# Max-pooling by 16 along rows: two load slots that swing over a 9.5 KB gap, in place of three fixed ones

## The chip, the cores and the metric

The kernel runs on one core of a Trainium2 chip, with nothing else on it. The metric is the device time of one execution in microseconds (us). All timed runs were at a granted clock of 1.0. Ratios are computed as the mean time of one kernel's runs over the mean of the other's in the same rounds, so they are not quite the ratio of the medians that the text quotes. "Same" means within 2%.

## The reference

```python
# x: (32, 256, 4096) float32, output_size = 256
for i in range(output_size):
    start = int(i * length / output_size)
    end = int((i + 1) * length / output_size)
    result[:, :, i] = np.max(x[:, :, start:end], axis=-1)
```

Every output is the maximum of 16 neighbouring numbers: 134.22 MB are read, 8.39 MB are written. Per SBUF partition there are 16,384 outputs. The text calls one output with its 16 inputs (64 bytes) a *column*.

## The kernel before

One SBUF area per partition holds three load slots at its low end and the results at its high end. Results grow downwards into the space of the slots, so the loads shrink: one of 128 columns, two of 1,024, then three each of 1,000, 940, 884, 832 and 784, and at the end 736 and 152.

```python
slot_sizes = [MOST]                     # MOST = 1024 columns, 64 KB
rounds = [[FIRST] + [MOST] * (SLOTS - 1)]     # FIRST = 128, SLOTS = 3
# ... each later round: three loads of what the free room allows ...
for i, size in enumerate(loads):
    # ...
    at = n_loads % SLOTS * slot_sizes[n_loads // SLOTS] * W
    slot = area[:, at : at + size * W]
    nc.sync.dma_start(out=slot, in_=xg[:, a * W : b * W])
    nc.vector.reduce_max(
        out=area[:, base + a : base + b],
        in_=slot.rearrange("p (n w) -> p n w", w=W),
        axis=mybir.AxisListType.X,
    )
# ... after all loads: three stores, all on SyncE
for dst, src in stores:
    nc.sync.dma_start(out=dst, in_=src)
```

A load waits until the reduction that last read its slot is finished. With three slots, a load that is issued then has one whole load queued ahead of it and the rest of another moving.

Of the kernel before, what the change touches and what calls it, by code (L numbers as in the profile page):

```python
# [1 line left out]

# [4 lines left out]


@with_exitstack
def kernel(  # L10
    ctx: ExitStack,
    tc: tile.TileContext,
    x: bass.AP,
    output_size: bass.AP,
    out: bass.AP,
):





    nc = tc.nc
    P = nc.NUM_PARTITIONS
    fp32 = mybir.dt.float32

    B, C, L = x.shape
    O = int(output_size)
    assert L % O == 0, (L, O)
    W = L // O
    total = B * C * O // P  # L30
    assert B * C * O % P == 0

    AREA = 53200
    SLOTS = 3
    MOST = 65536 // (4 * W)
    ALIGN = 4
    FIRST = 128
    ROUNDS_A = 3
    LAST = 4


    slot_sizes = [MOST]
    rounds = [[FIRST] + [MOST] * (SLOTS - 1)]
    left = total - sum(rounds[0])
    while left:
        room = AREA - (total - left)
        n = min(room // (SLOTS * W + SLOTS) // ALIGN * ALIGN, MOST)
        if left <= slot_sizes[-1]:
            n = left
        slot_sizes.append(n)  # L50
        rounds.append([])
        while left and len(rounds[-1]) < SLOTS:
            n = min(n, left)
            rounds[-1].append(n)
            left -= n
    sizes = [n for r in rounds for n in r]
    groups = [sizes[: ROUNDS_A * SLOTS], sizes[ROUNDS_A * SLOTS :]]

    pool = ctx.enter_context(tc.tile_pool(name="pool", bufs=1))
    area = pool.tile([P, AREA], fp32, tag="area", name="area")  # L60

    xw = x.flatten_outer_dims().rearrange("r (o w) -> (r o) w", w=W)
    ow = out.flatten_outer_dims().rearrange("r o -> (r o)")

    stores = []
    n_loads = 0
    first = 0
    low = AREA
    for g, loads in enumerate(groups):
        n = sum(loads)  # L70
        xg = xw[first : first + P * n].rearrange("(p n) w -> p (n w)", p=P)
        og = ow[first : first + P * n].rearrange("(p n) -> p n", p=P)
        first += P * n
        base = low - n
        b = n
        for i, size in enumerate(loads):
            a = b - size
            at = n_loads % SLOTS * slot_sizes[n_loads // SLOTS] * W
            slot = area[:, at : at + size * W]
            nc.sync.dma_start(out=slot, in_=xg[:, a * W : b * W])  # L80
            nc.vector.reduce_max(  # L81
                out=area[:, base + a : base + b],
                in_=slot.rearrange("p (n w) -> p n w", w=W),
                axis=mybir.AxisListType.X,
            )
            n_loads += 1
            b = a
        low = base
        if g < len(groups) - 1:
            stores.append((og, area[:, base : base + n]))  # L90
        else:
            end = sum(loads[len(loads) - LAST :])
            for a, b in ((end, n), (0, end)):
                stores.append((og[:, a:b], area[:, base + a : base + b]))

    for dst, src in stores:
        nc.sync.dma_start(out=dst, in_=src)


# [1 line left out]
_INS = ['x', 'output_size']  # L101
_OUTS = [((32, 256, 256), 'float32')]

_NUMBERS = {'output_size': 256}


# [26 lines left out]
```

## Time and profile before

| before | |
|---|---|
| time, median of the first 3 runs | 335.2 us (335.14 to 335.36) |
| span of the profiled run | 333.4 us |
| bytes moved | 142.61 MB, 428 GB/s over the span |
| DMA queue, share of 16 engines' span | 99.1% |
| VectorE busy | 276.0 us (83%), 20 reductions |

Lines of the page of before: busy times, the DMA queue table (packets, MB, share of 16 engines' span), bytes, and the chain that ended last (DVE is VectorE, POOL is GpSimd, DMA a wait for a transfer).

```profile
span 333.4 us, 112 instructions
DVE 276.0 (83%) x20; POOL 0.2 (0%) x4
...
q1 hardware_dynamic: 3312, 142.61, 99.1%
HBM read 134.22 MB, written 8.39 MB: 428 GB/s over the span
...
DMA 64%; DVE 31%; DVEq 1%; another core or an unknown queue 0%; SPq 0%; issue 0%
```

The DMA engines are occupied throughout. VectorE's 31% in the chain are releases of slots, which hide under loads that are already queued; they cost nothing as long as the queue is never empty. A sign that it never is: the timeline of before from 60 to 102 us (start, duration, engine, line, what, and in brackets the idle time before it and who ended it; SPq is SyncE's sequencer, which issues):

```profile
44.26 17.22 DVE L81 TENSOR_REDUCE area<-area 128x1024 f32<-128x16384 f32 x1 [2.33 <-DMA area<-in_x_dram]
61.51 37.81 SPq L80 DMA_DIRECT2D area<-in_x_dram  x3
63.17 16.82 DVE L81 TENSOR_REDUCE area<-area 128x1000 f32<-128x16000 f32 x1 [1.69 <-DMA area<-in_x_dram]
82.14 16.82 DVE L81 TENSOR_REDUCE area<-area 128x1000 f32<-128x16000 f32 x1 [2.15 <-DMA area<-in_x_dram]
100.96 16.82 DVE L81 TENSOR_REDUCE area<-area 128x1000 f32<-128x16000 f32 x1 [2.00 <-DMA area<-in_x_dram]
```

A reduction starts when its load has landed, so the starts show the pace of the loads: 8.192 MB (128 partitions x 16,000 x 4 bytes) every 18.8 to 19.0 us, about 433 GB/s. The load issued at 61.51 us is not needed before 82.14 us, when the load that is queued ahead of it has come in too: 20.6 us in advance.

### The profile page before, as it was taken

To read this page: it belongs to the slowest core of one execution; us is meant where nothing else is said; L and a number is where in the kernel's file an instruction comes from. 1 tells how busy PE (TensorE), PEld (TensorE's weight loads), DVE (VectorE), ACT (ScalarE), POOL (GpSimd) and SP (SyncE) were. 2 spreads that over 40 slices of the span, in tenths; PEclk is the share of its full clock that TensorE was granted. 3 is DMA by queue.
4 is the path that set the end of the run, shared out by engine and by line. 5 is a ranking of instruction groups with operands and counts; after the bars stand their busy time and mean duration, and the time that the engine had idled before them with its cause. 6 is when DMAs were issued, how large, how long until landed. Compare 5 with 4: busy or idle time off the path is not lost.

```text
span 333.4 us, 112 instructions
## 1 busy us (share of the span) xinstructions
DVE 276.0 (83%) x20; POOL 0.2 (0%) x4
## 2 busy tenths in 40 slices
DVE  2009979797988989797989797989898898989990
POOL 0000000000000000000000000000000000000000
DMA  9898989898999998999999999999999999989997
GB/s 377 377 503 377 503 369 491 369 491 369 491 397 433 462 462 375 433 462 441 434 434 434 434 434 415 409 441 473 415 409 470 397 470 397 470 380 452 414 431 310
DMA packets 3312, 142.61 MB, mean 428 GB/s; under 512 B 368, under 2 KB 368, under 8 KB 368
## 3 DMA queue, kind: packets, MB, share of 16 engines
q1 hardware_dynamic: 3312, 142.61, 99.1%
HBM read 134.22 MB, written 8.39 MB: 428 GB/s over the span
## 4 chain that ended last, share of the span: by engine, by line
DMA 64%; DVE 31%; DVEq 1%; another core or an unknown queue 0%; SPq 0%; issue 0%
DMA area<-in_x_dram 64%; DVE area L81 31%; DVEq L128 1%; SPq L80 0%; DVEq L81 0%
## 5 line engine op out<-in xcount | busy, mean ns | idle before, releaser
L81 DVE TENSOR_REDUCE area<-area 128x1000 f32<-128x16000 f32 (+8 forms) x20 | 276.0, 13806 | 49.1 <-DMA area<-in_x_dram 49.1
L114 POOL MEMSET const-bfloat16-1.0<- 128x1 bf16 x1 | 0.1, 102 | 0.0
L114 POOL MEMSET const-uint8-127<- 128x1 uint8 x1 | 0.1, 101 | 0.0
L114 POOL MEMSET const-float32-0.0<- 128x1 f32 x1 | 0.1, 99 | 0.2 <-issue 0.2
L114 POOL MEMSET const-float32-1.0<- 128x1 f32 x1 | 0.1, 98 | 0.0
## 6 DMA issues: line engine op xcount, KB each, us to landing
area<-in_x_dram SPq DMA_DIRECT2D x3, 8000.0 KB, 40.1
area<-in_x_dram SPq DMA_DIRECT2D x3, 7520.0 KB, 37.5
area<-in_x_dram SPq DMA_DIRECT2D x3, 7072.0 KB, 35.3
area<-in_x_dram SPq DMA_DIRECT2D x3, 6656.0 KB, 33.2
area<-in_x_dram SPq DMA_DIRECT2D x3, 6272.0 KB, 31.3
area<-in_x_dram SPq DMA_DIRECT2D x1, 5888.0 KB, 30.3
out_dram<-area SPq DMA_DIRECT2D x1, 3998.0 KB, 27.6
out_dram<-area SPq DMA_DIRECT2D x1, 2966.0 KB, 34.2
```

The costliest lines, as they stand in the source:

```text
L81: nc.vector.reduce_max(out=area[:, base + a : base + b], in_=slot.rearrange("p (n w) -> p n w", w=W), axis=mybir.AxisListType.X,)
L114: nc = _bacc.Bacc("TRN2", target_bir_lowering=False, num_devices=1)
L128: with _tile.TileContext(nc) as tc:
```

## The change

Its intent is fewer and equal loads (17 instead of 20) of the largest row, 64 KB per partition, in two slots instead of three. Beside two 64 KB slots and the results some 19 KB per partition are left. That room becomes a gap of 152 columns (9.5 KB) at each slot: successive loads of a slot lie alternately at its low and at its high end. Two of them overlap in 872 of 1,024 columns only. The reduction is cut in two: first the 872 columns that the next load will overwrite, then the other 152. So the next load may be issued while the second part is still being reduced. The short first load (132 columns) lies in the first slot's gap, and the last results in the last slot.

```diff
-    SLOTS = 3
-    MOST = 65536 // (4 * W)
-    FIRST = 128
+    CHUNK = 1024
+    GAP = 152
+    FIRST = 132
+    LOADS_A, LOADS_B = 9, 6
...
+                low = n_loads % 2 * (CHUNK + GAP)
+                moved = n_loads // 2 % 2
+                at = low + moved * GAP
+                nc.sync.dma_start(out=ring[:, at * W : (at + n) * W], in_=xn)
+                if n == CHUNK:
+                    cut = CHUNK - GAP if moved else GAP
+                    parts = [(0, cut), (cut, n)]
+                    for u, v in parts if moved else parts[::-1]:
+                        pooled(dst[:, u:v], at + u, v - u)
+                else:
+                    end = (at + CHUNK) * W
+                    last_kept = ring[:, end - n : end]
+                    pooled(last_kept, at, n)
...
+        stores.append((og[:, 0:full], kept[:, base : base + full]))
...
+    stores.append((og[:, full : full + last], last_kept))
     for dst, src in stores:
         nc.sync.dma_start(out=dst, in_=src)
```

`pooled` is the `reduce_max` of before. The three stores stay at the end of SyncE's queue.

More of the change, by code (lines that the diff above doesn't have):

```diff
@@ L31 @@
     assert B * C * O % P == 0
-    AREA = 53200
-    SLOTS = 3
-    MOST = 65536 // (4 * W)
-    ALIGN = 4
-    FIRST = 128
-    ROUNDS_A = 3
-    LAST = 4
-    slot_sizes = [MOST]
-    rounds = [[FIRST] + [MOST] * (SLOTS - 1)]
-    left = total - sum(rounds[0])
-    while left:
-        room = AREA - (total - left)
-        n = min(room // (SLOTS * W + SLOTS) // ALIGN * ALIGN, MOST)
-        if left <= slot_sizes[-1]:
-            n = left
-        slot_sizes.append(n)
-        rounds.append([])
-        while left and len(rounds[-1]) < SLOTS:
-            n = min(n, left)
-            rounds[-1].append(n)
-            left -= n
@@ L56 @@
-    sizes = [n for r in rounds for n in r]
-    groups = [sizes[: ROUNDS_A * SLOTS], sizes[ROUNDS_A * SLOTS :]]
+    CHUNK = 1024
+    GAP = 152
+    FIRST = 132
+    LOADS_A, LOADS_B = 9, 6
+    last = total - FIRST - (LOADS_A + LOADS_B) * CHUNK
+    assert 0 < last and last * (W + 1) <= CHUNK * W
     pool = ctx.enter_context(tc.tile_pool(name="pool", bufs=1))
-    area = pool.tile([P, AREA], fp32, tag="area", name="area")
+    ring = pool.tile([P, 2 * (CHUNK + GAP) * W], fp32, tag="ring", name="ring")
@@ L62, with pooled, group @@
+    kept = pool.tile([P, total - last], fp32, tag="kept", name="kept")
     xw = x.flatten_outer_dims().rearrange("r (o w) -> (r o) w", w=W)
     ow = out.flatten_outer_dims().rearrange("r o -> (r o)")
+    def pooled(dst, at, n):
+        nc.vector.reduce_max(
+            out=dst,
+            in_=ring[:, at * W : (at + n) * W].rearrange("p (n w) -> p n w", w=W),
+            axis=mybir.AxisListType.X,
+        )
+    taken = 0
+    def group(n):
+        nonlocal taken
+        span = slice(taken * P, (taken + n) * P)
+        taken += n
+        return (
+            xw[span].rearrange("(p n) w -> p (n w)", p=P),
+            ow[span].rearrange("(p n) -> p n", p=P),
+        )
@@ L65 @@
     stores = []
     n_loads = 0
-    first = 0
-    low = AREA
-    for g, loads in enumerate(groups):
-        n = sum(loads)
-        xg = xw[first : first + P * n].rearrange("(p n) w -> p (n w)", p=P)
-        og = ow[first : first + P * n].rearrange("(p n) -> p n", p=P)
-        first += P * n
-        base = low - n
-        b = n
-        for i, size in enumerate(loads):
-            a = b - size
-            at = n_loads % SLOTS * slot_sizes[n_loads // SLOTS] * W
-            slot = area[:, at : at + size * W]
-            nc.sync.dma_start(out=slot, in_=xg[:, a * W : b * W])
-            nc.vector.reduce_max(
-                out=area[:, base + a : base + b],
-                in_=slot.rearrange("p (n w) -> p n w", w=W),
-                axis=mybir.AxisListType.X,
-            )
-            n_loads += 1
-            b = a
-        low = base
-        if g < len(groups) - 1:
-            stores.append((og, area[:, base : base + n]))
-        else:
-            end = sum(loads[len(loads) - LAST :])
-            for a, b in ((end, n), (0, end)):
-                stores.append((og[:, a:b], area[:, base + a : base + b]))
+    base = 0
@@ new lines @@
+    for g, loads in enumerate(
+        ([FIRST] + [CHUNK] * LOADS_A, [CHUNK] * LOADS_B + [last])
+    ):
+        xg, og = group(sum(loads))
+        a = 0
+        for n in loads:
+            xn = xg[:, a * W : (a + n) * W]
+            dst = kept[:, base + a : base + a + n] if n != last else None
+            if n == FIRST:
+                nc.sync.dma_start(
+                    out=ring[:, CHUNK * W : (CHUNK + n) * W], in_=xn
+                )
+                pooled(dst, CHUNK, n)
+            else:
[8 more added lines that the diff above has]
+                        pooled(dst[:, u:v], at + u, v - u)
+                else:
+                    end = (at + CHUNK) * W
+                    last_kept = ring[:, end - n : end]
+                    pooled(last_kept, at, n)
+                n_loads += 1
+            a += n
+        full = a - last if g else a
+        stores.append((og[:, 0:full], kept[:, base : base + full]))
+        base += full
@@ L96 @@
+    assert taken == total
+    stores.append((og[:, full : full + last], last_kept))
     for dst, src in stores:
```

## The prediction

> **What bounds the kernel now.** The DMA engines, throughout. The page's queue table gives the one hardware queue 99.1% of 16 engines' span; 142.61 MB cross in 333.4 us, 428 GB/s. The Trainium skill, "DMA: Bandwidth & Descriptors", section "Where 436 GB/s comes from", puts the port ceiling at 435.2 GB/s; this trace agrees: loads of 8.192 MB land 18.9 us apart, 433.5 GB/s. 142.61 MB at 435.2 GB/s are 327.7 us, so 5.7 us are not pure transfer. By the timeline: about 3.0 us until data flow (reductions start at 5.22 and 24.7 us), 1.6 us spread over the 17 middle loads (0.09 us each), 0.4 us in the stores, 0.8 us of closing. VectorE is busy 276.0 us (83%) and waits 0.8 to 2.3 us for DMA before nearly every load (the waits view: 49.1 us, all DMA). The "DVE 31%" in the chain of waits is slot release, hidden under queued loads.
>
> **What the change does.** Same bytes, same engine, same queue.
> - Removes three loads (20 to 17). At 0.06 to 0.09 us per transfer: 0.2 us, all critical, since the queue is always busy.
> - Moves: three slots become two. A load may start when 872 columns of its slot's last load are reduced. From the trace's shapes (128 columns 2.286 us, 1024 columns 17.22 us) a reduction costs 0.15 us + 16.67 ns per column: 872 columns 14.7 us, 152 columns 2.7, together 17.4 us per load; 12 more instructions, 1.8 us more VectorE, hidden under a 64 KB load of about 19.35 us.
> - Queue depth. Landing + 14.7 us + about 1.1 us from issue to first data (first issue 0.73 us, first packets 1.74 us) is about 16 us after landing; the engines run dry at about 18.8 us (19.35 less a 0.58 us spread between the engines' landings). Margin about 2.7 us: no bubble. Without the gap it would be about 0.15 us.
> - Tail. The last load (892 columns, 16.9 us) lands 0.6 us before VectorE is done with the one before; its 15.0 us reduction ends about 15.7 us after landing, so the last store's data could flow at 16.8. The first two stores (7.93 MB, 18.3 us at the trace's store rate) cover that by about 1 us. The last store is smaller (0.46 instead of 1.26 MB), but store bytes are equal in all: the end doesn't move.
> - Start: the same three loads up front; a first load of 132 columns instead of 128 changes nothing on a queue that is busy from 1.74 us.
>
> **Prediction.** 335.2 - 0.2 = 335.0 us; range 334.6 to 336.0. Faster by over 2%: 0.01 (it needs under 328.5 us, almost the pure transfer time); within 2%: 0.97; slower by over 2%: 0.02.
>
> **What would show it.** Queue share about 99%; starts of the large reductions 19.3 to 19.4 us apart; VectorE idle about 1.9 us before each, released by DMA; loads issued 14.7 us after a landing; VectorE busy about 278 us. Wrong if landings are 20 us or more apart, or slices of the DMA row fall below 0.9.
>
> **What would make it wrong.** A slow issue with only one load queued ahead (15 boundaries; 0.5 us each would be 7.5 us); 64 KB rows being slower (the two in this trace landed 19.49 and 19.55 us apart, which I put down to engines drifting apart at the start; if not, 0.15 us x 15 = 2.3 us); a bad row pitch; the last store not covered.

## The result, and the profile after

The changed kernel takes 335.15 us (median of 6 runs, 335.02 to 335.32) against 335.19 us of before in the same rounds (335.11 to 335.36): ratio 0.9999, 95% interval 0.9987 to 1.0012. It is the same.

The same lines of the page of the changed kernel:

```profile
span 333.5 us, 112 instructions
DVE 276.5 (83%) x32; POOL 0.2 (0%) x4
...
q1 hardware_dynamic: 2880, 142.61, 99.1%
HBM read 134.22 MB, written 8.39 MB: 428 GB/s over the span
...
DMA 57%; DVE 40%; issue 0%; SPq 0%
```

Twelve more reductions cost VectorE 0.5 us, and 432 packets fewer were moved; bytes, rate and queue share are unchanged. VectorE's share of the chain grew from 31% to 40% and the time did not: this share says how the chain was followed, not what a faster engine would win.

The timeline of the changed kernel from 39 to 64 us:

```profile
24.94 17.28 DVE L52 TENSOR_REDUCE kept<-ring 128x872 f32<-128x13952 f32 x2 [16.99 <-DMA ring<-in_x_dram]
39.65 19.68 SPq L92 DMA_DIRECT2D ring<-in_x_dram  x2
44.29 17.28 DVE L52 TENSOR_REDUCE kept<-ring 128x872 f32<-128x13952 f32 x2 [2.08 <-DMA ring<-in_x_dram]
63.65 14.69 DVE L52 TENSOR_REDUCE kept<-ring 128x872 f32<-128x13952 f32 x1 [2.08 <-DMA ring<-in_x_dram]
```

The load issued at 39.65 us waited 14.71 us for the 872-column part of the reduction that began at 24.94. It is issued 4.64 us before the reduction of the one other load in flight starts (44.29). I call this the **lead**: the pace of the loads (19.35 us) less the hold from a reduction's start to the issue that it releases, here 19.35 - 14.71 = 4.64 us. The DMA engines have a little less than that: by the packet records of the trace the 16 engines end the load ahead 3.9 to 4.2 us after the issue, and its reduction starts 0.4 us after the last of them. Loads land 19.35 us apart, and the last store hides as well, as the end of the timeline of the changed kernel shows:

```profile
...
295.87 17.28 DVE L52 TENSOR_REDUCE kept<-ring 128x872 f32<-128x13952 f32 x2 [2.07 <-DMA ring<-in_x_dram]
313.10 15.02 DVE L52 TENSOR_REDUCE ring<-ring 128x892 f32<-128x14272 f32 x1
328.15 0.33 SPq L111 DMA_DIRECT2D out_dram<-ring  x1
```

The last reduction starts without idle time before it, because its load landed while VectorE still had work. The packet records of the trace show the second store's last packets ending at 330.34 to 330.96 us, and the last store's packets following without a pause.

So the number was right. The question for the experiments was whether the reasons were: what sets the time, how large the margin of the two slots really is, what a transfer costs, and what covers the tail.

### The profile page after: what moved, and what is told of

It reads as the page before. It is cut to its first block, busy times and chain, and to the rows that moved or that the text cites. A ratio compares the mean times of both kernels' runs of the same rounds, so it can differ in the third digit from the quotient of the medians.

```text
span 333.5 us, 112 instructions
## 1 busy us (share of the span) xinstructions
DVE 276.5 (83%) x32; POOL 0.2 (0%) x4
## 3 DMA queue, kind: packets, MB, share of 16 engines
q1 hardware_dynamic: 2880, 142.61, 99.1%
## 4 chain that ended last, share of the span: by engine, by line
DMA 57%; DVE 40%; issue 0%; SPq 0%
DMA ring<-in_x_dram 57%; DVE kept L52 36%; DVE ring L52 5%; SPq L83 0%
## 5 line engine op out<-in xcount | busy, mean ns | idle before, releaser
L52 DVE TENSOR_REDUCE kept<-ring 128x872 f32<-128x13952 f32 (+2 forms) x31 | 261.5, 8477 | 51.6 <-DMA ring<-in_x_dram 51.6
L52 DVE TENSOR_REDUCE ring<-ring 128x892 f32<-128x14272 f32 x1 | 15.0, 15019 | 0.0
```

The source lines that it names most:

```text
L52: nc.vector.reduce_max(out=dst, in_=ring[:, at * W : (at + n) * W].rearrange("p (n w) -> p n w", w=W), axis=mybir.AxisListType.X,)
```

## The experiments

Each is the changed kernel with the edit shown. "Hold" is read from a timeline as above (first undisturbed pair of loads), and the lead is 19.35 us less the hold.

### 1. VectorE almost free: one_of_16

```diff
-            in_=ring[...].rearrange("p (n w) -> p n w", w=W),
+            in_=ring[...].rearrange("p (n w) -> p n w", w=W)[:, :, 0:1],
```

Its output is wrong, which doesn't matter for the time.

> The changed kernel with every reduction cut to the first of the 16 elements (wrong result on purpose): VectorE work falls from 276 to about 20 us, loads are queued much earlier, nothing waits for VectorE. Theory that the DMA engines alone set the time: 334.9 to 335.3 us, the same. Rival (slot waits, reductions or their SBUF reads cost the stream something): 333 us or less.

Measured: 335.12 us, before 335.16, ratio 1.0004 (0.9992 to 1.0016). From its page:

```profile
span 333.2 us, 112 instructions
DVE 30.8 (9%) x32; POOL 0.2 (0%) x4
...
q1 hardware_dynamic: 2880, 142.61, 99.1%
```

With VectorE's work cut from 276.5 to 30.8 us (expected: about 20) and a lead of about 17.7 us the time stays. Neither slots nor reductions cost the changed kernel anything; 335 us is what the DMA engines need. The Trainium skill, "SBUF — State Buffer", section "Who interferes with whom", says that a DMA does not contend with a compute engine for SBUF; this run agrees to within 0.2%.

### 2. Two slots without the gap: nogap

```diff
-                moved = n_loads // 2 % 2
+                moved = 0
...
-                    cut = CHUNK - GAP if moved else GAP
-                    parts = [(0, cut), (cut, n)]
-                    for u, v in parts if moved else parts[::-1]:
-                        pooled(dst[:, u:v], at + u, v - u)
+                    pooled(dst, at, n)
```

> Two 64 KB slots that do not swing: a load waits for the whole 1024-column reduction (17.22 us) instead of its first 872 columns (14.69 us). Margin theory (the queue only has to be refilled before the engines run dry): landing + 17.2 + 1.1 to 1.6 us is just about the moment at which they run dry, so 335.1 to 336.0 us, loads landing 19.35 to 19.45 us apart. Rival (having only one load queued ahead costs at each boundary, and the gap is what makes two slots work): 0.5 us or more for each of 14 loads, 342 us or more.

Measured: 353.05 us (350.86 to 355.06), before 335.16: ratio 1.0541 (1.0509 to 1.0574). From its page, and then its timeline from 41 to 68 us:

```profile
span 351.1 us, 97 instructions
DVE 275.7 (79%) x17; POOL 0.2 (0%) x4
...
q1 hardware_dynamic: 2880, 142.61, 96.2%
```

```profile
24.96 17.22 DVE L52 TENSOR_REDUCE kept<-ring 128x1024 f32<-128x16384 f32 x1 [16.96 <-DMA ring<-in_x_dram]
42.21 19.75 SPq L92 DMA_DIRECT2D ring<-in_x_dram  x2
44.38 17.22 DVE L52 TENSOR_REDUCE kept<-ring 128x1024 f32<-128x16384 f32 x1 [2.20 <-DMA ring<-in_x_dram]
66.35 17.22 DVE L52 TENSOR_REDUCE kept<-ring 128x1024 f32<-128x16384 f32 x1 [4.74 <-DMA ring<-in_x_dram]
```

My theory had said 335 to 336 us: it fell in its size. The load issued at 42.21 us, with a lead of 2.1 us, landed at 66.35 us, 21.97 us after the one ahead and not 19.35. The packet records say how: 15 of the 16 DMA engines went on to this load at 43.66 to 44.06 us, almost without a pause; the sixteenth began it at 45.91, 3.7 us after the issue, and its first packet took 0.6 us longer than the usual 2.42 (those of most others were longer too, by up to 0.7). Where VectorE waits for a load in these traces, its reduction starts 0.3 to 0.6 us after the last engine's last packet, so one late engine delays the reduction, which delays the next issue. Such delays add up to 18 us over the run.

The page needs care here. Its queue share fell by 2.9 points only. 96.2% of 351.1 us are 337.8 us per engine, against 99.1% of 333.5, 330.5 us: of 17.6 us more span, 7.3 are longer packets, counted as busy, and 10.3 idle.

### 3. The lead, or the swing itself: nogap_short

The slots do not swing, but the hold is shortened: the 152 columns that are reduced last look at one element of 16. Its output is wrong, which doesn't matter for the time.

```diff
-                moved = n_loads // 2 % 2
+                moved = 0
...
+                    pooled(dst[:, GAP:n], at + GAP, n - GAP)
+                    nc.vector.reduce_max(out=dst[:, 0:GAP],
+                        in_=ring[...].rearrange("p (n w) -> p n w", w=W)[:, :, 0:1], ...)
```

> Two 64 KB slots that do not swing, as nogap, but the last 152 columns of each reduction look at the first of the 16 elements alone (wrong result on purpose), so a whole slot comes free about 15.0 us after landing instead of 17.2: loads are issued about 3.5 us before the first engine runs dry. Theory L (what cost nogap 18 us is the short lead alone, and the swing is worth exactly the lead it buys): 335.1 to 336.0 us, landings 19.35 us apart. Rival (loading into the same addresses over and over, or having two slots without a gap, costs by itself): 345 us or more.

Measured: 335.09 us, before 335.2, ratio 0.9999 (0.9985 to 1.0012). Its timeline from 39 to 45 us:

```profile
24.88 14.69 DVE L52 TENSOR_REDUCE kept<-ring 128x872 f32<-128x13952 f32 x1 [16.98 <-DMA ring<-in_x_dram]
39.48 0.40 DVE L95 TENSOR_REDUCE kept<-ring 128x152 f32<-128x152 f32 x1
39.91 0.33 SPq L92 DMA_DIRECT2D ring<-in_x_dram  x1
44.23 14.69 DVE L52 TENSOR_REDUCE kept<-ring 128x872 f32<-128x13952 f32 x1 [4.35 <-DMA ring<-in_x_dram]
```

With the same fixed slots and a lead of 4.32 us all 18 us are gone. It is the lead that counts. The swing is worth the lead that it buys; no other effect of it shows.

### 4. How much lead is needed: gap_d15, gap_d30, gap_d60, nogap_d60

An extra reduction of 15, 30 or 60 columns, its result unused, ahead of the work that releases the slot. For 60 columns on the swinging slots (on 15 and 30 alike):

```diff
+    scratch = pool.tile([P, 60], fp32, tag="scratch", name="scratch")
...
+                    pooled(scratch[:, :], at + GAP, 60)
                     parts = [(0, cut), (cut, n)]
```

and on the fixed slots of nogap, into a free part of the ring:

```diff
+                    free = (2 * CHUNK + GAP) * W + n_loads * 60
+                    pooled(ring[:, free : free + 60], at, 60)
                     pooled(dst, at, n)
```

> The changed kernel with the same extra 60-column reduction (1.15 us) ahead of the 872-column part: VectorE works 18.5 us per load, slots come free 15.9 us after landing, still about 1.5 us inside the margin. Margin theory: 335.1 us, same as the changed kernel within 0.3. The last reduction starts later by 1.1 us, which the tail's cover of about 1 us just allows: up to 336. Rival (VectorE's work itself slows the stream, or the change has no slack): 337 us or more.

> As nogap, with one extra 60-column reduction (1.15 us, result unused) ahead of each load's reduction: slots come free 18.4 us after landing, past the margin by 0.4 to 1.0 us. Margin theory: that excess shows once per two loads (two slots, each cycle of a slot is stretched), so 7 times 0.4 to 1.0 us: 338 to 342 us, with DMA engines idle between loads. Rival (only VectorE's total work counts: 18.4 us per load is still under 19.35): 335.2 us.

> The changed kernel with an extra 15-column reduction (about 0.4 us) ahead of the 872-column part, so each load is issued about 3.4 to 3.7 us before the engines run dry, instead of 3.85 to 4.2. Theory E (after the first batch: a load issued while the engines stream reaches the last of the 16 engines only some 4.2 to 4.8 us after its issue, so the changed kernel sits just at the edge): first stalls, 336 to 340 us, with landings of one or two engines up to 1 us late. Rival (1.1 to 1.6 us from issue to data as at the start; what cost 8 us in the run with 60 columns was something else, such as VectorE's load): 335.2 us.

> The changed kernel with an extra 30-column reduction (0.65 us) ahead of the 872-column part: loads issued about 3.0 to 3.3 us before the first engine runs dry, between the run with 15 columns (3.24 to 3.6 us, no late landing) and the run with 60 (2.6 us, +8 us). If the need for lead lies near 3 us, as those two say: some late landings, 336 to 341 us. If the steps are gradual from zero: about half of the 60-column run's excess, 339 us. If it needs under 2.9 us: below 336.2.

| run | hold, us | lead, us | time, us | before, same rounds | ratio (95%) |
|---|---|---|---|---|---|
| one_of_16 | 1.63 | 17.7 | 335.12 | 335.16 | 1.0004 (0.9992 to 1.0016) |
| the change | 14.71 | 4.64 | 335.15 | 335.19 | 0.9999 (0.9987 to 1.0012) |
| gap_d15 | 15.02 | 4.33 | 335.84 | 335.08 | 1.0020 (1.0008 to 1.0033) |
| nogap_short | 15.03 | 4.32 | 335.09 | 335.2 | 0.9999 (0.9985 to 1.0012) |
| gap_d30 | 15.28 | 4.07 | 337.81 | 335.24 | 1.0114 (1.0069 to 1.0160) |
| gap_d60 | 15.78 | 3.57 | 343.29 | 335.16 | 1.0259 (1.0237 to 1.0281) |
| nogap | 17.25 | 2.10 | 353.05 | 335.16 | 1.0541 (1.0509 to 1.0574) |
| nogap_d60 | 18.31 | 1.04 | 350.3 | 335.16 | 1.0476 (1.0432 to 1.0521) |

gap_d60 was to stay at 335.1 to 336 and took 343.29: the change has much less slack than 1.5 us. gap_d30 fell into its range, gap_d15 just below it (335.84, expected 336 to 340; nogap_short loses nothing at the same lead, so what its 0.8 us are made of is left open; in its profiled run, at 335.65 us, two early loads were through 19.5 us after the one ahead, which is 0.36 us in all). Down to a lead of 4.3 us at most 0.8 us are lost; at 4.07 it begins to cost, at 3.57 it costs 8 us. So the change stands 0.3 to 0.6 us before the edge (4.64 less 4.33, and less 4.07). The two holds at the edge, from the timelines of gap_d15 from 44 to 60 us and of gap_d30 from 25 to 42 us:

```profile
44.40 0.40 DVE L53 TENSOR_REDUCE scratch<-ring 128x15 f32<-128x240 f32 x1 [2.00 <-DMA ring<-in_x_dram]
...
59.42 0.33 SPq L93 DMA_DIRECT2D ring<-in_x_dram  x1
```

```profile
25.02 0.65 DVE L53 TENSOR_REDUCE scratch<-ring 128x30 f32<-128x480 f32 x1 [16.98 <-DMA ring<-in_x_dram]
...
40.30 0.33 SPq L93 DMA_DIRECT2D ring<-in_x_dram  x1
```

A late landing looks like this in the timeline of gap_d60 from 59 to 86 us:

```profile
...
60.27 19.68 SPq L93 DMA_DIRECT2D ring<-in_x_dram  x2
63.84 1.15 DVE L53 TENSOR_REDUCE scratch<-ring 128x60 f32<-128x960 f32 x1 [1.01 <-DMA ring<-in_x_dram]
64.91 17.27 DVE L53 TENSOR_REDUCE kept<-ring 128x872 f32<-128x13952 f32 x2
84.28 1.15 DVE L53 TENSOR_REDUCE scratch<-ring 128x60 f32<-128x960 f32 x1 [2.10 <-DMA ring<-in_x_dram]
...
```

The load issued at 60.27 us is reduced from 84.28 on, as if all of it had begun 19.35 us earlier, at 64.93, 4.7 us after the issue. By the packet records two engines paused and took it up at 63.53 and 63.75 us, 3.3 and 3.5 us after the issue; their first packets took 3.4 and 3.0 us instead of 2.42, and the 0.4 us from the last packet to the reduction come on top.

nogap_d60 missed its range (338 to 342) too, and it is the odd one: more delay, and by the medians less time. (The intervals of the two ratios touch, and its profiled run is its slowest, 354.49 us, so the trace cannot say why the median is lower.) There the first load with a short lead was issued at 43.25 us, about 1 us before the reduction of the one ahead (timeline of nogap_d60 from 40 to 47 us):

```profile
...
43.25 0.33 SPq L92 DMA_DIRECT2D ring<-in_x_dram  x1
44.29 1.15 DVE L52 TENSOR_REDUCE ring<-ring 128x60 f32<-128x960 f32 x1 [1.07 <-DMA ring<-in_x_dram]
45.36 17.21 DVE L52 TENSOR_REDUCE kept<-ring 128x1024 f32<-128x16384 f32 x1
```

By the packet records all 16 engines had ended the load ahead by 43.87 us, and all took the new one up at 44.21 to 44.63, 1.0 to 1.4 us after the issue. In nogap it was the same: where 14 engines or more had run dry, they began 0.95 to 2.0 us after the issue, and where one engine alone paused while the others streamed, it began 3.5 to 3.8 us after it. So in these runs engines that had run dry took a new load up sooner than the last engine of a streaming queue did. That VectorE's total work decides (the rival, 335.2 us) is out: in nogap_d60 VectorE worked 18.3 of 19.35 us per load, in gap_d60 about as much, and they differ by 7 us.

### 5. Are long packets the reason: nogap_rows16

As nogap, but each 64 KB row is written as four pieces of 16 KB with 256 bytes between them, in one transfer: packets of about 0.6 us.

```diff
+                rows = ring[:, at * W : (at + 4 * (q + 4)) * W].rearrange(
+                    "p (h m) -> p h m", h=4)[:, :, : q * W]          # q = n // 4
+                nc.sync.dma_start(out=rows, in_=xn.rearrange("p (h m) -> p h m", h=4))
```

> The kernel without gap, but each partition's 64 KB of a load are written as four pieces of 16 KB with 256 bytes between them, in one transfer: packets of about 0.6 us instead of 2.4 us. Theory P (a busy engine takes up the new load's work only between packets, so the late arrival grows with the packet): the last engine is served about 2.4 us or less after the issue, 336 to 340 us instead of 353. Rival Q (the late arrival is the time to hand out the work to busy engines, whatever its packet size, or grows with the number of packets): 350 us or more.

Measured: 353.58 us (352.49 to 354.94), before 335.08, ratio 1.0563 (1.0540 to 1.0585). I had supposed that a busy engine looks for new work only between packets. That theory fell: packets of a quarter of the length leave the time as it was. (Some 3 us of the 18.5 are the price of more packets, estimated from 0.22 us for each of 15 loads in section 6; about 15 us of stalls remain, where 1 to 5 were expected.) Why a load reaches the last engine so late while the engines stream is open; the runs show only that it happens, that the delay is shorter for engines that run dry, and that packet length is not its main reason. Nor does it happen every time: the last store of the change was issued 2.2 us before the first engine was through with the second store, and no engine paused.

### 6. What a transfer costs: split4

```diff
-                nc.sync.dma_start(out=ring[:, at * W : (at + n) * W], in_=xn)
+                q = n // 4
+                for i in range(4):
+                    nc.sync.dma_start(out=ring[:, (at + i * q) * W : (at + (i + 1) * q) * W],
+                                      in_=xn[:, i * q * W : (i + 1) * q * W])
```

> The changed kernel with every load but the first issued as four transfers of 256 columns: 65 loads instead of 17, rows of 16 KB. Measures the cost of a transfer that I predicted 0.06 to 0.09 us for the change's saving. If that is right, and no stall comes: 48 more transfers cost 2 to 4.5 us, 337 to 340 us. If the cost is per byte alone: 335.2. The first quarter is issued as early as before, the last 1.3 us later.

Measured: 339.09 us, before 335.08, ratio 1.0118 (1.0104 to 1.0132): 48 more transfers cost 4.0 us, 0.083 us each, inside the 0.06 to 0.09 us that I had assumed. But they are not the transfers' own cost. In nogap_rows16, which has the same 16 KB rows without one transfer more, the first two large loads landed 19.57 us apart, as its timeline from 20 to 66 us shows:

```profile
25.10 17.22 DVE L100 TENSOR_REDUCE kept<-ring 128x1024 f32<-128x16384 f32 x1 [17.21 <-DMA ring<-in_x_dram]
42.35 19.94 SPq L96 DMA_DIRECT2D ring<-in_x_dram  x2
44.67 17.22 DVE L100 TENSOR_REDUCE kept<-ring 128x1024 f32<-128x16384 f32 x1 [2.35 <-DMA ring<-in_x_dram]
...
```

That is 0.22 us over 19.35. One such pair proves little, since first pairs with 64 KB rows took from 19.35 us (the change) to 19.59 (gap_d15). But the packet records agree: from 6 to 42 us, before the first load that had to wait for its slot, 8.4 MB took 19.50 us in nogap_rows16, 19.49 in split4 and 19.32 in the change. In split4 the pace is as slow: 39.15 us for two loads (reductions at 83.84 and 122.99 us in its timeline), 19.58 each. One row per partition is eight packets per engine (128 partitions on 16 engines), so four rows are 24 packets more: 0.18 to 0.22 us / 24, 8 to 9 ns a packet. The change saved three transfers, 24 packets per engine, again 0.2 us by this estimate.

### 7. What covers the tail: early_store and early_store_act

```diff
+                if n_loads == 11:
+                    dst_a, src_a = stores.pop()
+                    nc.sync.dma_start(out=dst_a, in_=src_a)      # nc.scalar in early_store_act
```

> The changed kernel with the first store (4.79 MB, 11.0 us) issued in the stream, after the twelfth 64 KB load, instead of after the last load. The same bytes on the same queue, but the last load's reduction (15.0 us, ending about 15.7 us after landing) is now covered by 7.3 us of stores instead of 18.3. Tail theory: the engines idle 8.5 to 10 us before the last store, 343.5 to 345.5 us. Rival (where the stores stand does not matter, only the bytes): 335.2 us.

> As early_store, with the first store issued from ScalarE's queue, so that its 4.79 MB can run beside a load instead of between two. If the 16 engines are one shared capacity whatever the queue and the direction: the loads beside it land later by the same 11 us in all, 344.5 to 345.5 us as early_store. If a store from SBUF and a load into SBUF can overlap in an engine: 334 to 340 us.

Measured: early_store 345.01 us, before 335.08, ratio 1.0294 (1.0280 to 1.0308), as expected. The end of its timeline:

```profile
...
324.76 15.01 DVE L52 TENSOR_REDUCE ring<-ring 128x892 f32<-128x14272 f32 x1
324.88 0.34 SPq L114 DMA_DIRECT2D out_dram<-kept  x1
339.80 0.34 SPq L114 DMA_DIRECT2D out_dram<-ring  x1
```

The last reduction and what precedes it are the same. But only the second store, 3.15 MB or 7.3 us, is left to run under it, from 324.88 us at the earliest, and the engines then wait for the last store until 339.80 us. Holding all stores back to the end is worth 10 us here.

early_store_act: 345.62 us, before 335.24, ratio 1.0312 (1.0298 to 1.0326), 0.1 us above its range and 0.6 from early_store. The queue table of its page has two queues:

```profile
q1 hardware_dynamic: 2736, 137.82, 92.9%
q10 hardware_dynamic: 144, 4.79, 3.4%
HBM read 134.22 MB, written 8.39 MB: 415 GB/s over the span
```

A second queue and the other direction add no capacity: the load beside the store came later instead (reductions at 199.14 and 230.89 us, 31.75 apart and not 19.35). The Trainium skill, "DMA: Bandwidth & Descriptors", section "Rules for kernel authors", says that spreading DMAs over SP, ACT and GpSimd does not help, since they run on the same 16 engines; this run agrees.

### 8. The first load: first128

```diff
-    FIRST = 132
+    FIRST = 128
```

> The changed kernel with a first load of 128 columns as before (the last load takes the other 4: 896). In every trace of a kernel with 132 columns the first load landed 5.45 to 5.68 us after the start, in the one of before 5.20; 4 columns more are worth 0.08 us. Theory S (the 132-column rows of 8,448 bytes or the layout that comes with them give back 0.2 to 0.3 us at the start, and that is where the saving of three transfers went): first landing at 5.2 us, 334.8 to 335.0 us. Rival (scatter of the start): landing 5.4 us or later and 335.1 us.

Measured: 334.83 us (334.71 to 335.45), before 335.24, ratio 0.9992 (0.9980 to 1.0005). The first reduction began at 5.54 us, as late as in the runs with 132 columns (5.59 in the change, 5.22 in before), which speaks for the rival, while the time is the one of theory S. The interval includes 1. Inconclusive: the fastest median, and not a shown gain.

## Why the prediction was right or wrong

**The time: right.** 335.15 us were measured, 335.0 predicted, inside 334.6 to 336.0 and inside "within 2%".

**DMA engines bound the kernel throughout: shown for the changed kernel,** where taking VectorE nearly away (one_of_16) changed nothing. For before no run took VectorE away; the same queue share, 99.1%, the same time and a load issued 20.6 us in advance speak for it. The expected 0.2 us is not visible as a difference: the interval is 0.4 us wide on either side. split4 confirms the rate it was worked out with, and nogap_rows16 adds that most of it goes with the packets and not with the transfers.

**VectorE's side: right.** Pace 19.35 us (predicted 19.3 to 19.4), idle time 2.07 us before each load's reduction (1.9), issue 14.7 us after the reduction's start (14.7), 276.5 us busy (278: the two parts of a reduction overlap a little, 17.28 us together where I added 17.4).

**The tail: right.** The last store followed without a pause, and early_store took 9.9 us more, where the missing cover gave 8.5 to 10.

**The step that failed: "Queue depth".** "About 1.1 us from issue to first data", "Margin about 2.7 us: no bubble", "Without the gap it would be about 0.15 us". I took 1.1 us from the first issue of the execution, when all engines are idle and the first of them begins. For engines that have run dry it holds (1.0 to 1.4 us in nogap_d60). What counts is the last of 16 engines while they stream: by the packet records it began 3.5 to 3.8 us after the issue in nogap and up to 4.2 us after it in gap_d60. (The 4.7 us worked out from a landing in section 4 also contain the longer packets and the 0.4 us to the reduction.) The form of the argument holds (a load must be in the queue before the engines run dry: nogap_short), but the term was too small by 2.4 to 3.1 us in those cases. The conclusion "no bubble" survived by 0.3 to 0.6 us of lead, not 2.7, and that it survived was luck: the sum did not show how near the edge was. Without the gap the loss is 18 us, not nothing.

**"What would make it wrong" named the right risk**, a slow issue with only one load queued ahead. The other one, 64 KB rows being slower, did not come: 64 KB loads landed 19.35 us apart all along, and the 19.49 and 19.55 us of the trace before were the start.

## What to carry to other kernels

When a DMA queue sets the time, as here, two slots do as well as three and a nearly free engine behind them wins nothing, until a load is issued later than some lead before the engines run dry; beyond that edge a few tenths of a microsecond per load turned into per cents. Measure that lead on streaming engines, by adding small delays to the release of a slot, and not from the first transfer of a trace; here it is a little over 4 us with 8.4 MB loads, counted to the next reduction. A slot that swings over a small gap, with the overlapping part reduced first, is a cheap way to buy lead where memory for a third slot is missing.

## What the Trainium skill lacked or had wrong

- "DMA: Bandwidth & Descriptors", section "Latency and other measured facts", gives about 600 ns to the first byte of a DMA from the SyncE queue. Here the first packets came 1.0 us after the first issue began (0.73 to 1.74 us); counted from the end of that issue, which took 0.38 us, it is 0.63 us, so the figure fits if it is meant so. For a load issued into a streaming queue, an engine that paused alone began 3.5 to 3.8 us after the issue (nogap). No page gives a figure for that case, and it decided 18 us here.
- The same page, section "Where 436 GB/s comes from": the ceiling of 435.2 GB/s agrees. The 64 KB loads of the change land at 433.5 GB/s (8.389 MB in 19.35 us), and the whole execution runs at 428.
- The same page, section "Rules for kernel authors", asks for 1 MiB or more per DMA. The rule names no row length (a cost per packet stands elsewhere on the page), and the row length still counts above 1 MiB: 2 MiB transfers with 16 KB rows took 19.58 us per 8.4 MB against 19.35 us with 64 KB rows, about 9 ns per packet and engine.
- No page says that stalls come with longer packets, which count as busy: nogap is 17.6 us longer, and 7.3 us of that are longer packets.
